# Transposes in place of diagonal products, and GpSimd work in the attention, in a two-layer diffusion backbone

## The chip, the cores and the metric

The kernel runs on one core of a Trainium2 chip. The metric is the device time of one execution in microseconds; smaller is better. Before the change three runs gave a median of 1726.25 us (1725.76 to 1727.16).

## What is computed

Two layers of a diffusion backbone work on 256 latent tokens (one batch) with 256 context tokens as a prefix, 1024 features each, in float32. Each layer is a half-step SwiGLU, a token mixer, and a second half-step SwiGLU. Layer 0 mixes with a bidirectional gated linear recurrence, layer 1 with windowed attention of 16 heads over 4 key heads, with rotary angles and a sink per head.

```python
def rms_norm(x, g):
    return x * rsqrt(mean(x * x, -1) + 1e-6) * g

def modulate(h, g_pre, shift, scale):
    return rms_norm(h, g_pre) * (1 + scale) + shift

def half_ffn_update(h, mod, k, g_pre, g_post, w_in, w_out):
    y = swiglu(modulate(h, g_pre, mod[3*k], mod[3*k+1]), w_in, w_out)
    return h + 0.5 * mod[3*k+2] * rms_norm(y, g_post)

for each layer:
    x, ctx = half_ffn_update(...)            # both streams
    x, ctx = x + gate * rms_norm(mixer(modulate(x, ...), modulate(ctx, ...)), g)
    x, ctx = half_ffn_update(...)            # the last layer: x alone
```

In the attention a softmax over latent keys within a window of 128, all context keys and the sink gives the weights p, and the output is p times the values.

## The kernel before

The 512 tokens lie in four tiles of 128 (0 and 1 context, 2 and 3 latent), always taken in the order 2, 3, 0, 1. The residual `x` lies in SBUF with tokens on the partitions. A matmul wants the features on the partitions, so each tile is normed, turned and modulated before a layer uses it.

**Products in two parts.** A float32 operand is split into a rounded part `hi` (ScalarE, `copy` in L112) and the remainder `lo` (VectorE, subtraction in L113), and each product is the sum of three matmuls (L135 to L137, L150 to L152). Weights arrive by DMA in slots of 128x1024 (`wslot`, L115) and are split the same way; there are 5 slots for raw weights and 8 for split ones.

**Norm and turn.** `mean_sq` (L154) takes the squares' sum on ScalarE and writes the squares into a scratch tile; `rstd` (L159) takes the inverse root in eight tiny VectorE instructions. `diag` (L176) makes a 128x128 diagonal matrix of it, and `turn` (L181) multiplies each 128x128 block of `x` by that diagonal matrix on TensorE, which norms and turns it in one product. The results lie in PSUM, four blocks to a bank. `pre_turn` (L216) applies scale and shift (ScalarE, L225) and splits the result into `hh` and `hl`. `first_turn` (L240) does it for the first layer.

**Boundaries.** After a tile's last output product, `post` (L190) norms the output and adds it to `x`; `pre` (L204) norms the new `x` with high priority and puts off the turning by some matmul units (`DELAY`, `tick`). There are four boundaries with four tiles each, two latent tiles at the end of the attention, and the four tiles of the start: 22 in all.

**The attention** (`attn_mixer`, L718). Eight projection units of 128 query columns, each followed by `rotate` (L757: two products, a permutation matmul and a sum in L768), two of keys, and four tiles of values. Then eight steps: `soft` (L827) computes the scores of four heads, their maximum, exponential and row sums; `mix` (L852) makes four diagonal matrices of the inverse sums (L856), multiplies blocks of the weights by them on TensorE (L861), which scales and turns them, splits the result, and multiplies by the values (L867, L868). The code asks for the scores of step s before the mixing of step s-1. `proj` multiplies by the output weights. GpSimd issues some DMAs and has no arithmetic.

**Order.** The order on each engine is fixed when the program is built, by a scheduler that takes ready instructions by priority. Each engine works through its queue in that order and waits on semaphores.

Of the kernel before, what the change touches and what calls it, by code (L numbers as in the profile page):

```python
# [7 lines left out]
F32 = mybir.dt.float32  # L8
# [3 lines left out]
ALU = mybir.AluOpType  # L12
# [3 lines left out]
P = 128  # L16
# [17 lines left out]
RS = -1.0 / 8192.0  # L34


class Net:
    def __init__(self, ctx, tc):
        self.tc = tc
        self.nc = tc.nc  # L40
        self.ctx = ctx
        self.n = 0
        self.pending = []
        e = ctx.enter_context
        self.const = e(tc.tile_pool(name="const", bufs=1))
        self.big = e(tc.tile_pool(name="big", bufs=1))
        self.rawp = e(tc.tile_pool(name="rawp", bufs=5))
        self.wp = e(tc.tile_pool(name="wp", bufs=8))
        self.sm = e(tc.tile_pool(name="sm", bufs=10))
        self.tp = e(tc.tile_pool(name="tp", bufs=2))  # L50
        self.mmp = e(tc.tile_pool(name="mmp", bufs=4, space=PSUM))
        self.stp = e(tc.tile_pool(name="stp", bufs=4, space=PSUM))
        self.x = self.big.tile([P, 4, D], F32, name="xres")
        self.y = self.big.tile([P, 4, D], F32, name="y")
        self.hh = self.big.tile([P, NK, T], F32R, name="hh")
        self.hl = self.big.tile([P, NK, T], F32R, name="hl")
        self.dh = self.big.tile([P, NK, T], F32R, name="dh")
        self.dl = self.big.tile([P, NK, T], F32R, name="dl")
        self.ph = e(tc.tile_pool(name="ph", bufs=1))
        self.rows = {}  # L60

    def nm(self, s):
        self.n += 1
# [51 lines left out]
    def wslot(self, srcs):  # L115
        nc = self.nc
        raw = self.raw()
        n = 0
        for s in srcs:
            a, b = s.shape[1:]  # L120
            nc.sync.dma_start(raw[:, n : n + a * b].rearrange("p (a b) -> p a b", b=b), s)
            n += a * b
        hi = self.wp.tile([P, D], F32R, tag="whi", name=self.nm("whi"))
        lo = self.wp.tile([P, D], F32R, tag="wlo", name=self.nm("wlo"))
        self.split(hi[:, :n], lo[:, :n], raw[:, :n])
        return hi, lo

    def unit(self, out, w, nk, mh, ml, cols, kb=0, ws=P, wo=0):
# [44 lines left out]
            r = r2  # L173
        return r

    def diag(self, r):  # L176
        dg = self.sm.tile([P, P], F32, tag="diag", name=self.nm("diag"), bufs=2)
        self.nc.vector.tensor_scalar(dg, self.ident, r, RS, op0=ALU.mult, op1=ALU.mult)  # L178
        return dg

    def turn(self, t, b, dg):  # L181
        ps = self.st()
        for q in range(4):
            k = 4 * b + q
            self.nc.tensor.matmul(  # L185
                ps[:, q * P : (q + 1) * P], self.x[:, t, k * P : (k + 1) * P], dg, start=True, stop=True
            )
        return ps

    def post(self, t, ysrc, grow):  # L190
# [10 lines left out]
            nc.vector.scalar_tensor_tensor(tmp, ysrc, r, grow[cond], op0=ALU.mult, op1=ALU.mult)  # L201
        nc.vector.tensor_tensor(self.x[:, t], self.x[:, t], tmp, op=ALU.add)

    def pre(self, t, A, S):  # L204
        with self.tc.high_priority():
            dg = self.diag(self.rstd([self.mean_sq(self.tmp(), self.x[:, t])]))
        self.pending.append([DELAY[t], lambda: self.pre_turn(t, A, S, dg)])

    def tick(self, n):
        for p in list(self.pending):  # L210
# [2 lines left out]
                self.pending.remove(p)  # L213
                p[1]()

    def pre_turn(self, t, A, S, dg):  # L216
        nc = self.nc
        cond = t // 2
        tk = slice(t * P, (t + 1) * P)
        hf = self.tmp()  # L220
        for b in range(2):
            ps = self.turn(t, b, dg)
            for q in range(4):
                k = 4 * b + q
                nc.scalar.activation(  # L225
# [12 lines left out]
        return self.y.rearrange("p a (b t) -> p (a b) t", t=T)  # L238

    def first_turn(self, t):  # L240
        dg = self.diag(self.rstd([self.mean_sq(self.tmp(), self.x[:, t])]))
        for b in range(2):
            ps = self.turn(t, b, dg)
            self.nc.vector.tensor_copy(
                self.turned()[:, 4 * b : 4 * b + 4, t * P : (t + 1) * P], ps.rearrange("p (q c) -> p q c", c=P)
            )
# [183 lines left out]
def net_kernel(  # L430
# [102 lines left out]

        return step

    def boundary(grow, l2, k2, conds=(0, 1)):
        st = {}

        def after(t, ysrc):
            if not st:  # L540
                st["A"] = N.pre_cols(l2, k2, conds)
            with tc.high_priority():
                N.post(t, ysrc, grow)
            N.pre(t, *st["A"])

        return after

# [3 lines left out]
    def ffn(l, k, jobs, l2, k2, mid=None):  # L551
# [19 lines left out]
        1,  # L571
    )
    after_attn = {}
    attn_mixer(
        N,
        attn_w_qkv[0],
# [3 lines left out]
        k_rope,  # L580
        k_mask,
        lambda: after_attn.update(N.load_rows((1, 5), {1: N.x[:, 0]})),
        boundary(after_attn, 1, 2, (1,)),
    )
    last_ffn(N, ffn_w_in[1, 1], ffn_w_out[1, 1], N.load_rows((1, 8), {1: N.x[:, 1]}), out)


# [130 lines left out]
def attn_mixer(N, w_qkv, w_o, sink, k_perm, k_rope, k_mask, rows, after):  # L718
# [38 lines left out]
    def rotate(src):  # L757
# [7 lines left out]
        dst, t = a[:, :HT], a[:, HT:]  # L765
        v.tensor_tensor(dst, src, rope[:, 0], op=ALU.mult)
        v.tensor_tensor(t, pr[:, :HT], rope[:, 1], op=ALU.mult)
        v.tensor_tensor(dst, dst, t, op=ALU.add)  # L768
        return dst

    def qview(i):
# [79 lines left out]

    def mix(u, pts, rs):  # L852
        qt, g = u // NKV, u % NKV
        dg = consts[:, u % 2].rearrange("p (i q) -> p i q", q=P)
        for i in range(4):
            v.tensor_scalar(dg[:, i], N.ident, rs[:, i : i + 1], None, op0=ALU.mult)  # L856
        po = N.st()
        for k in range(4):
            tp = N.st()
            for i in range(4):  # L860
                nc.tensor.matmul(  # L861
                    tp[:, i * P : (i + 1) * P], pts[i][:, k * P : (k + 1) * P], dg[:, i], start=True, stop=True
                )
            ph = N.s2(F32R)
            pl = N.a2(F32R)
            N.split(ph, pl, tp)
# [174 lines left out]
```

## Time and profile before

| what | value |
|---|---|
| median of three runs | 1726.25 us |
| the profiled execution: its time, its span | 1725.57 us, 1723.8 us |
| TensorE busy, weight loads beside it | 1678.0 us (97%), 1425.6 us |
| VectorE busy | 1139.6 us (66%) |
| ScalarE busy | 716.5 us (42%) |
| GpSimd busy | 40.3 us (2%) |
| mean granted TensorE clock | 0.993 |

Busy is the time in which an engine had an instruction under way. Matmuls overlap one another, so the pace of TensorE is read from the distance of their starts. A line of the trace names the code line, the engine and the tiles as out<-in.

### The profile page before, as it was taken

The numbers are of one execution on the slowest core, as the hardware profiler recorded it, in microseconds if no ns is written. First come the engines' busy times: TensorE is split into PE (matmuls) and PEld (weight loads), VectorE is DVE, ScalarE is ACT, GpSimd is POOL, SyncE is SP. The second block draws the span as 40 slices with busy tenths as digits, with TensorE's granted clock in tenths as the row PEclk, the third lists the DMA queues.
The fourth block names the chain that finished last, engine by engine and source line by source line (L and its number), as shares of the span: only waits on it lengthen the run. The fifth ranks groups of instructions, "written<-read, shape, count | busy, mean of one in ns | idle before, by whom it ended". The sixth has DMA issues, their size and how long they took to land.

```text
span 1723.8 us, 23005 instructions
## 1 busy us (share of the span) xinstructions
PE 1678.0 (97%) x8980; PEld 1425.6 (83%) x8980; DVE 1139.6 (66%) x1798; ACT 716.5 (42%) x1148; POOL 40.3 (2%) x82
## 2 busy tenths in 40 slices
PE   5999999999999999999999999999999999999998
PEld 3988888788988798888888898788888887879997
DVE  4947778667878795777833685564433799765554
ACT  3423322225799362333232542322222576564442
POOL 0010000000000001000000001000000000000000
PEclk9999999999999999999999999999999999999999
DMA  9627655453223154666643165765432250047661
GB/s 333 207 92 235 214 171 172 148 170 97 87 86 98 50 192 145 204 190 206 175 119 97 50 190 169 241 220 182 112 106 86 63 181 27 1 141 216 189 188 38
DMA packets 261405, 253.58 MB, mean 147 GB/s; under 512 B 9792, under 2 KB 214040, under 8 KB 261296
## 3 DMA queue, kind: packets, MB, share of 16 engines
q1 hardware_dynamic: 256800, 244.35, 45.6%
q0 software_dynamic: 3456, 6.98, 1.3%
q8 instruction: 70, 1.15, 0.3%
q10 hardware_dynamic: 1040, 0.77, 0.1%
q14 instruction: 39, 0.32, 0.1%
HBM read 250.97 MB, written 1.10 MB: 146 GB/s over the span
## 4 chain that ended last, share of the span: by engine, by line
PE 78%; DVE 9%; ACT 6%; DMA 4%; issue 3%; ACTq 0%; DVEq 0%
PE mm L136 15%; PE mm L135 15%; PE mm L137 15%; PE mm L150 7%; PE mm L152 7%; PE mm L151 7%; DVE m L309 2%; DMA raw<-in_ffn_w_in_dram 2%; DVE wlo L113 2%; PE st L861 2%; PE st L185 1%; ACT tmp L225 1%; ACT whi L112 1%; DMA raw<-in_ffn_w_out_dram 1%; PE st L315 1%
## 5 line engine op out<-in xcount | busy, mean ns | idle before, releaser
L135 PE MATMUL mm<-hh,whi 128*128 128x512 f32 (+1 forms) x1808 | 614.0, 340 | 3.1 <-ACT hh L255 1.6
L136 PE MATMUL mm<-hl,whi 128*128 128x512 f32 (+1 forms) x1808 | 613.4, 340 | 2.0 <-DVE hl L257 1.5
L137 PE MATMUL mm<-hh,wlo 128*128 128x512 f32 (+1 forms) x1808 | 613.5, 340 | 1.0 <-DVE wlo L113 1.0
L112 ACT CAST whi<-raw 128x1024 fp32r<-128x1024 f32 x322 | 331.4, 1038 | 517.5 <-PE mm L136 244.8
L113 DVE TENSOR_TENSOR wlo<-raw,whi 128x1024 fp32r<-128x1024 f32 x322 | 382.6, 1202 | 204.9 <-ACT whi L112 202.2
L135 PEld LDWEIGHTS mm<-hh,whi 128*128 128x128 f32 x1808 | 343.6, 190 | 48.3 <-ACT whi L112 4.2
L136 PEld LDWEIGHTS mm<-hl,whi 128*128 128x128 f32 x1808 | 344.0, 190 | 39.8 <-DVE hl L257 2.1
L137 PEld LDWEIGHTS mm<-hh,wlo 128*128 128x128 f32 x1808 | 344.3, 190 | 38.3 <-DVE wlo L113 1.4
L309 DVE SCALAR_TENSOR_TENSOR m<-raw,cs,m 128x1024 f32<-128x1024 f32 x224 | 278.1, 1279 | 49.1 <-DMA raw<-in_w_mod_dram 37.8
L150 PE MATMUL mm<-whi,dh 128*128 128x512 f32 x592 | 233.3, 394 | 4.7 <-ACT dh L112 2.4
L152 PE MATMUL mm<-whi,dl 128*128 128x512 f32 x592 | 232.1, 392 | 0.4 <-DVE dl L113 0.4
L151 PE MATMUL mm<-wlo,dh 128*128 128x512 f32 x592 | 231.5, 391 | 0.0
L150 PEld LDWEIGHTS mm<-whi,dh 128*128 128x128 f32 x592 | 112.0, 189 | 33.9 <-issue 3.4
L357 DVE TENSOR_TENSOR a<-s,mm 128x512 f32<-128x512 f32 (+1 forms) x96 | 54.4, 567 | 128.2 <-PE mm L137 114.4
L152 PEld LDWEIGHTS mm<-whi,dl 128*128 128x128 f32 x592 | 111.9, 189 | 24.5 <-DVE dl L113 0.8
L151 PEld LDWEIGHTS mm<-wlo,dh 128*128 128x128 f32 x592 | 111.9, 189 | 22.7
L112 ACT CAST dh<-a 128x512 fp32r<-128x512 f32 (+1 forms) x96 | 50.6, 527 | 122.9 <-DVE a L357 122.8
L356 ACT ACTIVATE s<-mm 128x512 f32<-128x512 f32 (+1 forms) x96 | 48.0, 500 | 96.4 <-PE mm L137 96.1
L113 DVE TENSOR_TENSOR dl<-a,dh 128x512 fp32r<-128x512 f32 (+1 forms) x96 | 54.4, 567 | 18.9 <-ACT dh L112 18.6
L225 ACT ACTIVATE tmp<-st,modT,A 128x128 f32<-128x128 f32 x144 | 54.7, 464 | 7.0 <-PE st L185 7.0
L185 PE MATMUL st<-diag,xres 128*128 128x128 f32 x352 | 46.9, 289 | 6.8 <-DVE diag L178 6.2
L185 PEld LDWEIGHTS st<-diag,xres 128*128 128x128 f32 x352 | 44.7, 201 | 10.4 <-issue 6.2
(195 smaller groups left out, 1398.2 us busy)
## 6 DMA issues: line engine op xcount, KB each, us to landing
raw<-in_ffn_w_in_dram SPq DMA_DIRECT2D x176, 512.0 KB, 4.5
raw<-in_w_mod_dram SPq DMA_DIRECT2D x128, 512.0 KB, 4.2
raw<-in_ffn_w_out_dram SPq DMA_DIRECT2D x82, 512.0 KB, 4.5
wm<-in_w_mod_dram SPq DMA_DIRECT2D x16, 512.0 KB, 7.5
raw<-in_rg_w_in_dram SPq DMA_DIRECT2D x16, 512.0 KB, 4.7
raw<-in_attn_w_qkv_dram SPq DMA_DIRECT2D x12, 512.0 KB, 4.1
g<-spill POOLq DMA_DIRECT2D x16, 256.0 KB, 4.1
raw<-in_rg_gate_w_dram SPq DMA_DIRECT2D x16, 256.0 KB, 2.9
```

The costliest lines, as they stand in the source:

```text
L112: self.nc.scalar.copy(hi, src)
L113: self.nc.vector.tensor_tensor(lo, src, hi.bitcast(F32), op=ALU.subtract)
L135: nc.tensor.matmul(out, a, xh, start=(k == 0), stop=False)
L136: nc.tensor.matmul(out, a, xl, start=False, stop=False)
L137: nc.tensor.matmul(out, b, xh, start=False, stop=(k == nk - 1))
L150: nc.tensor.matmul(out, a, wh, start=(k == 0), stop=False)
L151: nc.tensor.matmul(out, a, wl, start=False, stop=False)
L152: nc.tensor.matmul(out, b, wh, start=False, stop=(k == nk - 1))
L185: self.nc.tensor.matmul(ps[:, q * P : (q + 1) * P], self.x[:, t, k * P : (k + 1) * P], dg, start=True, stop=True)
L225: nc.scalar.activation(hf[:, k * P : (k + 1) * P], ps[:, q * P : (q + 1) * P], AF.Identity, bias=S[:, k, cond : cond + 1], scale=A[:, k, c ...
L309: v.scalar_tensor_tensor(acc[c], raw, self.cs[:, k, c : c + 1], acc[c], op0=ALU.mult, op1=ALU.add)
L357: nc.vector.tensor_tensor(b, a, pu, op=ALU.mult)
```

## The change

The tile is scaled by VectorE into a copy and turned by plain transposes, in place of products with a diagonal matrix. At the boundaries the copy goes into `y`, elsewhere into a scratch tile. In the attention, too, transposes take the place of products with diagonal matrices; GpSimd scales the softmax weights in place, subtracts for the remainders `lo` of the weights of that stage, and takes the last sum of the rotation.

```diff
+        self.lo_eng = self.nc.vector
...
-        self.split(hi[:, :n], lo[:, :n], raw[:, :n])
+        nc.scalar.copy(hi[:, :n], raw[:, :n])
+        self.lo_eng.tensor_tensor(lo[:, :n], raw[:, :n], hi[:, :n].bitcast(F32), op=ALU.subtract)
...
-    def diag(self, r):
-        dg = self.sm.tile([P, P], F32, tag="diag", name=self.nm("diag"), bufs=2)
-        self.nc.vector.tensor_scalar(dg, self.ident, r, RS, op0=ALU.mult, op1=ALU.mult)
-        return dg
-
-    def turn(self, t, b, dg):
+    def scaled(self, t, xs):
+        r = self.rstd([self.mean_sq(xs, self.x[:, t])])
+        self.nc.vector.tensor_scalar(xs, self.x[:, t], r, RS, op0=ALU.mult, op1=ALU.mult)
+        return xs
+
+    def turn(self, xs, b):
         ps = self.st()
         for q in range(4):
             k = 4 * b + q
-            self.nc.tensor.matmul(
-                ps[:, q * P : (q + 1) * P], self.x[:, t, k * P : (k + 1) * P], dg, start=True, stop=True
-            )
+            self.nc.tensor.transpose(ps[:, q * P : (q + 1) * P], xs[:, k * P : (k + 1) * P], self.ident)
...
-    def pre(self, t, A, S):
+    def pre(self, t, A, S, buf):
         with self.tc.high_priority():
-            dg = self.diag(self.rstd([self.mean_sq(self.tmp(), self.x[:, t])]))
-        self.pending.append([DELAY[t], lambda: self.pre_turn(t, A, S, dg)])
+            xs = self.scaled(t, buf)
+        self.pending.append([DELAY[t], lambda: self.pre_turn(t, A, S, xs)])
...
     def first_turn(self, t):
-        dg = self.diag(self.rstd([self.mean_sq(self.tmp(), self.x[:, t])]))
+        xs = self.scaled(t, self.tmp())
...
-    def boundary(grow, l2, k2, conds=(0, 1)):
+    def boundary(grow, l2, k2, conds=(0, 1), keep=False):
...
-            N.pre(t, *st["A"])
+            N.pre(t, *st["A"], N.tmp() if keep else N.y[:, t])
...
+    N.lo_eng = nc.gpsimd
     attn_mixer(
...
-        boundary(after_attn, 1, 2, (1,)),
+        boundary(after_attn, 1, 2, (1,), True),
     )
+    N.lo_eng = v
...
-        v.tensor_tensor(dst, dst, t, op=ALU.add)
+        nc.gpsimd.tensor_tensor(dst, dst, t, op=ALU.add)
...
     def mix(u, pts, rs):
         qt, g = u // NKV, u % NKV
-        dg = consts[:, u % 2].rearrange("p (i q) -> p i q", q=P)
         for i in range(4):
-            v.tensor_scalar(dg[:, i], N.ident, rs[:, i : i + 1], None, op0=ALU.mult)
+            nc.gpsimd.tensor_scalar(pts[i], pts[i], rs[:, i : i + 1], None, op0=ALU.mult)
...
-                nc.tensor.matmul(
-                    tp[:, i * P : (i + 1) * P], pts[i][:, k * P : (k + 1) * P], dg[:, i], start=True, stop=True
-                )
+                nc.tensor.transpose(tp[:, i * P : (i + 1) * P], pts[i][:, k * P : (k + 1) * P], N.ident)
```

## Rows read from the trace of the kernel before

**Rows 1.** The page: busy us (share of the span) and instructions, TensorE to GpSimd

```profile
PE 1678.0 (97%) x8980; PEld 1425.6 (83%) x8980; DVE 1139.6 (66%) x1798; ACT 716.5 (42%) x1148; POOL 40.3 (2%) x82
```

**Rows 2.** Windows: us, busy PE, PEld, DVE, ACT, POOL, granted clock, DMA share, GB/s

```profile
0.00:35.00 35.00, 17.31 (x107) 9.72 (x108) 12.88 (x50) 8.00 (x14) 1.33 (x6) 0.94 0.98 338
...
1360.00:1426.00 66.00, 65.33 (x443) 59.20 (x442) 61.13 (x131) 50.70 (x96) 2.17 (x4) 1.00 0.50 160
1426.00:1512.00 86.00, 81.85 (x486) 69.42 (x485) 73.00 (x200) 55.68 (x131) 0.00 (x0) 1.00 0.07 21
```

**Rows 3.** Groups, whole run: line, out<-in, count | busy us, mean ns | idle before

```profile
L185 PE MATMUL st<-diag,xres 128*128 128x128 f32 x352 | 46.9, 289 | 6.8 <-DVE diag L178 6.2 <-issue 0.5
...
L861 PE MATMUL st<-m,y 128*128 128x128 f32 x256 | 35.9, 274 | 0.0
...
L178 DVE TENSOR_SCALAR diag<-ident,small 128x128 f32<-128x128 f32 x22 | 6.3, 286 | 0.5
...
L671 DVE TENSOR_SCALAR g<-g 128x512 f32<-128x512 f32 x16 | 6.1, 423 | 2.2 <-ACT g L669 2.2
...
L686 DVE TENSOR_TENSOR_SCAN g<-m,a 128x512 f32<-128x512 f32 x4 | 4.9, 1218 | 0.0
...
L688 DVE TENSOR_TENSOR_SCAN g<-m,s 128x256 f32<-128x256 f32 x4 | 2.7, 664 | 0.0
...
L795 DVE COPY y<-m 128x256 f32<-128x256 f32 x2 | 0.6, 283 | 0.0
```

**Rows 4.** The chain that ended last: start us, us, what

```profile
13.92 3.67 PE st L185 x16
...
393.18 1.78 PE st L185 x16
...
1439.37 1.11 PE st L861 x10
```

**Rows 5.** Timeline of TensorE at a group of transposes: start us, us

```profile
1207.49 0.60 PE L264 MATMUL st<-ident,s 128*128 128x128 f32 x4
1207.85 0.48 PE L150 MATMUL mm<-whi,dh 128*128 128x512 f32 x1
```

**Rows 6.** Groups of VectorE from 1360 to 1426 us

```profile
L113 DVE TENSOR_TENSOR wlo<-raw,whi 128x1024 fp32r<-128x1024 f32 x18 | 21.7, 1218 | 0.2 <-ACT whi L112 0.2
L786 DVE TENSOR_TENSOR dh<-m,dh 64x256 fp32r<-64x256 f32 x16 | 6.7, 420 | 0.5
L768 DVE TENSOR_TENSOR m<-m 128x256 f32<-128x256 f32 x10 | 4.2, 419 | 0.1
...
L113 DVE TENSOR_TENSOR hl<-tmp,hh 128x512 fp32r<-128x512 f32 x6 | 4.1, 688 | 0.3 <-ACT hh L112 0.2
L805 DVE TENSOR_TENSOR dl<-y,dl 64x512 fp32r<-64x512 f32 x6 | 4.1, 685 | 1.3 <-ACT dl L803 1.3
...
L170 DVE SCALAR_TENSOR_TENSOR small<-small,small 128x1 f32<-128x1 f32 x12 | 2.6, 216 | 0.2
L201 DVE SCALAR_TENSOR_TENSOR tmp<-y,small,g 128x1024 f32<-128x1024 f32 x2 | 2.6, 1286 | 0.1
L202 DVE TENSOR_TENSOR xres<-xres,tmp 128x1024 f32<-128x1024 f32 x2 | 2.4, 1217 | 0.0
...
L172 DVE SCALAR_TENSOR_TENSOR small<-small,small 128x1 f32<-128x1 f32 x12 | 1.9, 158 | 0.3
```

**Rows 7.** Groups of VectorE from 1426 to 1512 us

```profile
L856 DVE TENSOR_SCALAR m<-ident,soft 128x128 f32<-128x128 f32 x32 | 7.7, 279 | 0.1
L113 DVE TENSOR_TENSOR wlo<-raw,whi 128x1024 fp32r<-128x1024 f32 x5 | 6.1, 1217 | 0.0
```

**Rows 8.** Waits from 1426 to 1512 us: us in total, times, longest

```profile
ACT s L112 <- PE st L861: 17.3, 22, 1.7
```

More of the change, by code (lines that the diff above doesn't have):

```diff
@@ L214, in tick, with pre_turn @@
                 p[1]()
-    def pre_turn(self, t, A, S, dg):
+    def pre_turn(self, t, A, S, xs):
         nc = self.nc
@@ L221, in pre_turn @@
         for b in range(2):
-            ps = self.turn(t, b, dg)
+            ps = self.turn(xs, b)
             for q in range(4):
@@ L240, in first_turn @@
     def first_turn(self, t):
-        dg = self.diag(self.rstd([self.mean_sq(self.tmp(), self.x[:, t])]))
+        xs = self.scaled(t, self.tmp())
         for b in range(2):
-            ps = self.turn(t, b, dg)
+            ps = self.turn(xs, b)
             self.nc.vector.tensor_copy(
```

## The prediction

> **What bounds it now.** I read the page's busy shares first: TensorE is busy 1678.0 us of 1723.8, VectorE 1139.6 [rows 1]. In such a kernel a microsecond taken out of TensorE's queue is a microsecond gained, unless TensorE then waits for something else. So I next looked for what TensorE does in the lines the change touches [rows 3], at what pace [rows 4, 5], and then, stage by stage, whether another engine is near its limit [rows 2]. The reader should see there that from 1360 to 1426 us (last tile boundary, projections of the attention) VectorE works 61.1 of 66 us beside TensorE's 65.3, and from 1426 to 1512 us (scores and mixing) 73.0 of 86 beside 81.9. These two stages have two limits at once; elsewhere TensorE has the lead. The profiled execution took 1725.57 us, 0.7 under the median of 1726.25; I make the sum against it and add 0.7.
>
> **Diagonal products become transposes.** Each product has two TensorE instructions in the trace: 22 tiles x 8 products give the 352 of L185, 8 steps x 16 the 256 of L861 [rows 3]. In the chain of waits 16 of L185 take 1.78 us and 10 of L861 1.11 us, 0.111 us each [rows 4]. The transposes that are already there (L264) have one instruction each: four are begun at 1207.49 and the next matmul at 1207.85, 0.09 us each, and I count the 0.111 of the others, the smaller gain [rows 5]. One instruction in two goes.
> - 18 tiles (two context tiles, 16 at boundaries): 18 x 8 x 0.111 = 16.0 us off.
> - The last two tiles, in and behind the attention: 1.8 us off.
> - The mixing: 128 x 0.111 = 14.2 us off. That work is on the path: ScalarE waits 17.3 us for L861 in this stage [rows 8].
> - The first two tiles run at the low level of the clock (3.67 us for 16 instead of 1.78 [rows 4]), so 1.9 us could go in each; but the DMA share is 0.98 in that stretch [rows 2], and what follows waits for loads. Between 0 and 3 us; I take 1.
> Sum: 33.0 us off TensorE's queue.
>
> **Scaling the tile.** The 128x128 diagonal (L178, 286 ns) becomes a 128x1024 tensor_scalar on VectorE. The nearest rows of single-input forms are 283 ns at 256 columns (L795) and 423 at 512 (L671), 0.55 ns a column [rows 3]: 286 + 896 x 0.55 = 0.78 us, 0.49 more per tile. The far bound is a 1024-column instruction with two inputs, 1.29 us (L201 [rows 6]), 1.00 more. Behind it TensorE's first bank of four is ready 0.45 us sooner than with products, so the chain into the next layer keeps its length; and the work lies under the next tile's matmuls except at the last tile. Cover is gone where VectorE is full. I take 1 us for all 22 tiles, bounds 0 and 10. The squares' scratch moving from tmp to y costs nothing: y[t] was read for the last time just before.
>
> **Work moved to GpSimd in the attention.** The trace has no arithmetic on GpSimd, so I bound it. Low end: VectorE's own times, 1.22 us for a weight difference, 0.42 for the rotary sum [rows 6], 0.42 for a 512-column scaling (L671 [rows 3]). High end: the slowest element rate among the elementwise rows, the scan, 1218 ns for 512 columns and 664 for 256 [rows 3], so 2.44, 0.66 and 1.22 us. As the trace shows nothing faster for this engine, I take the high end. The Trainium skill ("GPSIMD Engine Reference", section 3.1) gives 1.96 times VectorE's time for a two-input add; by it a difference would take an estimated 2.4 us, the same sum.
> - 1360 to 1426: 18 differences and 10 sums, 43.9 + 6.6 = 50.5 us of GpSimd in 66. VectorE loses 21.7 + 4.2 us [rows 6] and gains 2 x 0.49: 36 us left. The differences were split far ahead of their use, so 1.2 us more latency is covered; if that lead is used up TensorE waits about a difference, 1.2 us.
> - 1426 to 1512: 32 scalings and the last 2 differences of the output weights (the other 3 of the 5 shown belong to the next layer), 39 + 5 = 44 us in 86. VectorE loses the 32 diagonals, 7.7 us [rows 7], and 2.4: 63 us left. The four scalings stand in series before a step's transposes, 4.9 us instead of 1.1; they lie under the scores of the next head group, as mixing trails the scores by one step. GpSimd's queue also holds the row loads that wait for the residual tiles; those are free sooner now, since the transposes read the copy.
> The relief can remove at most TensorE's idle time in the two stages, 0.7 + 4.1 us. Against that stands a conflict over memory between VectorE and GpSimd, which no row here shows: together bounds of 5 off and 22 on (below). I take 4 on, nearer to the idle time that the rows do show: the order on each engine is planned anew, and the scalings are a new wait.
>
> **Sum:** -33.0 + 1 + 4 = -28; 1725.6 - 28 + 0.7 = **1698 us**.
>
> **Rivals.**
> *VectorE and GpSimd lock each other out for instructions with two inputs in SBUF.* In 1360 to 1426 there are 56 such left on VectorE (L786, hl of L113, L805, L170, L172, L201, L202), 24.4 us in all [rows 6]. If each meets a GpSimd instruction in 50.5/66 of cases and waits half a difference (1.22 us), that is 52 us: 36 + 52 = 88 against 66, so 22 us on, while at half of that nothing is lost. Without the 1.8 us of the stage's own two tiles: 1725.6 - 31 + 1 + 22 - 2 = 1716 us with the rest as in the sum but the small relief. Against it: the 6 output-weight differences in this stage aren't needed until 1460 us and can slip. The Trainium skill ("SBUF — State Buffer", section "Who interferes with whom") states just this exclusion, a whole instruction long; no run here shows it, and by that rule 1716 would come out where I forecast 1698. Chance 0.23.
> *GpSimd costs nothing in the path* and the relief closes the gaps: -33 + 1 - 5: 1689 us. Chance 0.1.
> *Slower: GpSimd and VectorE exclude each other for every instruction.* Place: the two attention stages. Price: 36 + 50.5 = 87 in 66 us and 63 + 44 = 107 in 86, so 42 us on, and the 17.8 us saved in them void: 1726 - 15 + 42 = 1753 us. It decides from the point where both stages together grow by over 15 us. Against it: most of VectorE's time in the second stage goes to instructions that read a matmul result, not SBUF alone. Chance 0.04.
> *The clock falls.* In both stages the granted clock is 1.00, the level of 2.4 GHz [rows 2], with products and a few transposes between full-width matmuls. At 1.2 GHz the remaining 60 us or so of matmul work in the second stage would take 120: 1726 - 17 + 34 = 1743 us. The Trainium skill ("TensorE: Matmul & The Clock Gate", Part 4) says that transposes don't count as TensorE activity for the clock, which speaks against this change; by that rule the mixing would lose what keeps the clock up. The L264 groups here are too short to bear it out, but matmuls stand between all groups. Chance 0.01.
> *A transpose takes two instructions after all*, and nothing changes: 1726 us; against it stands the single instruction of the transposes there now [rows 5]. Chance 0.02.
>
> **How the numbers follow.** A difference under 0.2% (3.5 us) can't be told from none. The forecast has 0.6, over 1690 to 1708 us by its own bounds; the range reaches to 1687 for the free GpSimd and to 1715, most of the way to the lock, leaving out about 0.2. Faster: 0.6 + 0.23 + 0.1 = 0.93; same 0.02, the case without change; slower 0.04 + 0.01 = 0.05.
>
> **What would show it.** Right: 176 instructions of L185's successor and 128 of L861's at 0.11 us; a tile's scaling near 0.78 us; the boundaries nearer together by 3.6 us per layer; the stretch from the first score to the last transpose down from 86 us to 70 to 78; the clock still 1.00. Wrong: VectorE's small instructions (L170, L786) longer or apart while GpSimd works, TensorE waiting for a GpSimd difference or scaling, weight splits late at the boundaries behind the longer scaling. The forecast is wrong above all if the two attention stages don't shrink together by some 12 us.

## The result, and the profile after

The changed kernel takes 1774.6 us (median of 4 runs, 1774.38 to 1778.49) against 1726.0 us for the kernel before on the same chip: a ratio of 1.029, interval 1.0277 to 1.0303. It is 49 us slower where 28 us faster was forecast.

The page's busy shares after, TensorE to GpSimd, beside [rows 1]:

```profile
PE 1672.4 (94%) x8676; PEld 1406.6 (79%) x8676; DVE 1148.0 (65%) x1736; ACT 717.6 (40%) x1148; POOL 146.4 (8%) x144
```

304 matmul instructions have gone (8980 before), as many as counted: 176 of the turns and 128 of the mixing. Yet TensorE is busy only 5.6 us less, in a span that grew by 49 us. Both say that the engine waited, and that part of its work ran at a lower clock. The windows of [rows 2], in the kernel after:

```profile
1360.00:1426.00 66.00, 46.18 (x270) 42.61 (x269) 52.93 (x77) 37.97 (x72) 41.54 (x25) 0.82 0.42 128
1426.00:1512.00 86.00, 67.79 (x339) 52.40 (x338) 53.09 (x121) 43.83 (x99) 46.83 (x30) 0.88 0.13 37
```

TensorE fell from 65.3 to 46.2 us of the 66, and VectorE too is idle more than before. Two engines that both lose busy time are waiting for a third or for each other. The granted clock fell from 1.00 to 0.82 and 0.88.

To find where the 49 us are, I read five marks from the timeline of TensorE in both kernels: the first turn of the first layer boundary, the first turn of the last one, the first score product, the start of the last value product, the end.

| stretch, us | before | after | difference |
|---|---|---|---|
| start to the first boundary | 393.0 | 392.7 | -0.3 |
| layers, up to the last boundary | 953.6 | 957.0 | +3.4 |
| last boundary and projections | 79.9 | 105.9 | +26.0 |
| eight steps of scores and mixing | 87.9 | 109.9 | +22.0 |
| rest | 209.4 | 207.2 | -2.2 |

So there are three things to explain: two losses of over 20 us in the attention, and layers that do not gain though 96 products, two instructions of 0.11 us each, became transposes of one there.

**The new instructions.** Groups of GpSimd, whole run (line, engine, operation, shapes, count | busy us, mean ns | idle before):

```profile
L857 POOL TENSOR_SCALAR y<-y,soft 128x512 f32<-128x512 f32 x32 | 50.2, 1585 | 46.2 <-DVE soft L851 35.2 <-ACT s L113 5.6 <-PE mm L840 5.4
L127 POOL TENSOR_TENSOR wlo<-raw,whi 128x1024 fp32r<-128x1024 f32 x20 | 48.7, 2448 | 120.4 <-ACT whi L126 110.6 <-issue 9.8
...
L770 POOL TENSOR_TENSOR m<-m 128x256 f32<-128x256 f32 x10 | 7.5, 752 | 11.9 <-DVE small L167 5.6 <-DVE m L769 4.1 <-PE mm L139 2.2
```

A difference takes 2.45 us (2.44 counted), a rotary sum 0.75 (0.66 counted), a scaling 1.59 us, above the high end of 1.22.

**The projections.** Groups of VectorE from 1349 to 1456 us:

```profile
L788 DVE TENSOR_TENSOR dh<-m,dh 64x256 fp32r<-64x256 f32 x16 | 17.3, 1082 | 7.0 <-ACT dh L787 6.7
L172 DVE SCALAR_TENSOR_TENSOR small<-small,small 128x1 f32<-128x1 f32 x18 | 13.3, 737 | 0.6
L114 DVE TENSOR_TENSOR hl<-tmp,hh 128x512 fp32r<-128x512 f32 x8 | 8.3, 1038 | 0.7 <-ACT hh L113 0.7
L174 DVE SCALAR_TENSOR_TENSOR small<-small,small 128x1 f32<-128x1 f32 x18 | 8.0, 445 | 0.6
...
L769 DVE TENSOR_TENSOR m<-st,m 128x256 f32<-128x256 f32 x10 | 4.2, 424 | 3.8 <-PE st L766 3.2
L114 DVE TENSOR_TENSOR a<-mm,s 128x256 fp32r<-128x256 f32 x10 | 4.2, 422 | 2.0 <-ACT s L113 1.8
```

Compare the means with [rows 6]: L788 (L786 before) has gone from 420 to 1082 ns, L172 (L170) from 216 to 737, L174 (L172) from 158 to 445, the split into hl from 688 to 1038. These four groups alone grew by 28 us. L769 and the split into `a` have the same operation, but one input is a matmul's result (st, mm); they kept 424 and 422. Of the groups in this stretch only such with both inputs in SBUF got longer, and in them only the instructions that meet one of GpSimd: seven of the 16 of L788 do and take 0.83 to 2.45 us, the other nine 0.42. The timelines of GpSimd and of VectorE show why (start us, us, instruction):

```profile
1378.28 7.05 POOL L127 TENSOR_TENSOR wlo<-raw,whi 128x1024 fp32r<-128x1024 f32 x3
```

```profile
1379.39 0.15 DVE L169 TENSOR_SCALAR small<-small 128x1 int32<-128x1 int32 x1
1379.58 5.77 DVE L172 SCALAR_TENSOR_TENSOR small<-small,small 128x1 f32<-128x1 f32 x1
1385.39 0.16 DVE L174 SCALAR_TENSOR_TENSOR small<-small,small 128x1 f32<-128x1 f32 x1
1385.58 0.22 DVE L172 SCALAR_TENSOR_TENSOR small<-small,small 128x1 f32<-128x1 f32 x1
```

An instruction on 128 numbers, 0.22 us long elsewhere, lasts 5.77 us. It begins 1.3 us into a row of three GpSimd differences and ends when the third does; GpSimd is not slowed. The one-input instruction ahead of it (L169) passed in 0.15 us in the midst of the first difference.

What TensorE waits for from 1349 to 1456 us (us in total, times, longest) is VectorE above all; it has no wait for a GpSimd difference there:

```profile
PE st L766 <- DVE a L114: 11.1, 4, 5.4
PE st L187 <- DVE y L180: 7.4, 2, 4.2
```

ScalarE waits 10.0 us for GpSimd's rotary sums, where it waited 4.2 for VectorE's. The rotary sum was not moved by itself in any run; with the differences alone on GpSimd (below) ScalarE waits 10.2 us for VectorE's sums, so the longer wait needs no sum on GpSimd.

**The steps.** Waits from 1456 to 1566 us (us in total, times, longest), beside [rows 8]:

```profile
ACT s L113 <- PE st L862: 31.2, 17, 6.7
PEld st L862 <- POOL y L857: 26.5, 21, 3.1
PE st L862 <- POOL y L857: 19.0, 20, 2.7
```

TensorE waits 19 us for GpSimd's scalings, and ScalarE, which needs the transposes next, waits 31.2 us where it waited 17.3. Four scalings of 1.59 us in series are 6.3 us ahead of a step's transposes.

**The layers.** TensorE at the end of a boundary (timeline):

```profile
630.04 0.28 PE L139 MATMUL mm<-hh,wlo 128*128 128x256 f32 x1
631.99 1.09 PE L187 MATMUL st<-ident,y 128*128 128x128 f32 x8 [1.67 <-DVE y L180]
635.10 1.22 PE L137 MATMUL mm<-hh,whi 128*128 128x256 f32 x4 [2.01 <-ACT hh L113]
...
637.66 0.41 PE L138 MATMUL mm<-hl,whi 128*128 128x256 f32 x1
637.87 0.41 PE L139 MATMUL mm<-hh,wlo 128*128 128x256 f32 x1
...
641.84 0.28 PE L137 MATMUL mm<-hh,whi 128*128 128x256 f32 x1
641.96 0.28 PE L138 MATMUL mm<-hl,whi 128*128 128x256 f32 x1
```

It waits 1.67 us for the scaled tile and 2.01 us for what follows the turn. Behind these waits the products come 0.21 us apart, and from 641.71 us 0.12 us. The windows of these stretches give a granted clock of 0.53 and then 1.00:

```profile
637.00:642.00 5.00, 5.00 (x25) 5.00 (x26) 2.87 (x3) 0.08 (x1) 0.00 (x0) 0.53 0.51 152
642.00:650.00 8.00, 8.00 (x70) 8.00 (x68) 4.35 (x5) 3.65 (x5) 0.00 (x0) 1.00 0.54 167
```

So these waits cost more again behind them, in work at the lower level of the clock (1.2 in place of 2.4 GHz).

### The profile page after: what moved, and what is told of

Its sections match the earlier page's. It is cut to its first block, busy times and chain, and to the rows that moved or that the text cites. A ratio compares the mean times of both kernels' runs of the same rounds, so it can differ in the third digit from the quotient of the medians.

```text
span 1772.7 us, 22478 instructions
## 1 busy us (share of the span) xinstructions
PE 1672.4 (94%) x8676; PEld 1406.6 (79%) x8676; DVE 1148.0 (65%) x1736; ACT 717.6 (40%) x1148; POOL 146.4 (8%) x144
## 5 line engine op out<-in xcount | busy, mean ns | idle before, releaser
L127 DVE TENSOR_TENSOR wlo<-raw,whi 128x1024 fp32r<-128x1024 f32 (+1 forms) x302 | 358.5, 1200 | 207.5 <-ACT whi L126 205.1
L137 PEld LDWEIGHTS mm<-hh,whi 128*128 128x128 f32 x1808 | 348.9, 194 | 52.7 <-ACT hh L113 4.5
L138 PEld LDWEIGHTS mm<-hl,whi 128*128 128x128 f32 x1808 | 348.7, 193 | 39.3 <-DVE hl L114 1.3
L139 PEld LDWEIGHTS mm<-hh,wlo 128*128 128x128 f32 x1808 | 348.6, 193 | 38.0 <-DVE wlo L127 0.9
L127 POOL TENSOR_TENSOR wlo<-raw,whi 128x1024 fp32r<-128x1024 f32 x20 | 48.7, 2448 | 120.4 <-ACT whi L126 110.6
L857 POOL TENSOR_SCALAR y<-y,soft 128x512 f32<-128x512 f32 x32 | 50.2, 1585 | 46.2 <-DVE soft L851 35.2
```

Of the source, the lines that this page charges most:

```text
L127: self.lo_eng.tensor_tensor(lo[:, :n], raw[:, :n], hi[:, :n].bitcast(F32), op=ALU.subtract)
L137: nc.tensor.matmul(out, a, xh, start=(k == 0), stop=False)
L138: nc.tensor.matmul(out, a, xl, start=False, stop=False)
L139: nc.tensor.matmul(out, b, xh, start=False, stop=(k == nk - 1))
L857: nc.gpsimd.tensor_scalar(pts[i], pts[i], rs[:, i : i + 1], None, op0=ALU.mult)
```

## The experiments

Four kernels split the change; only the rotary sum is in none of them alone. The theory going in: GpSimd's differences lock VectorE; its scalings are late; the turns' gain is lost in waits for VectorE.

**The turns alone.**

```
 after.py, with the attention of before:
-    N.lo_eng = nc.gpsimd
-        nc.gpsimd.tensor_tensor(dst, dst, t, op=ALU.add)
+        v.tensor_tensor(dst, dst, t, op=ALU.add)
 and mix() as before (diagonal products)
```

> The tile turns alone: scaled copy and transposes at the 22 tiles; the attention as before, nothing on GpSimd. Theory (the boundary's chain through VectorE sets when the last tile can be turned, so TensorE waits for what it saves): no gain, 1722 to 1732 us, with TensorE waiting over 1 us before the turn of the last context tile at three or more boundaries. Rival (TensorE's queue sets the time at the boundaries, and the loss in the changed kernel comes back from elsewhere): 1726 - 18 = 1708 us.

1737.6 us against 1726.6, ratio 1.0065 (1.0046 to 1.0083): slower than even the theory had it (1722 to 1732). The layers took 959.1 us in place of 953.6.

**The weight differences alone.**

```
 before.py, wslot():
-        self.split(hi[:, :n], lo[:, :n], raw[:, :n])
+        nc.scalar.copy(hi[:, :n], raw[:, :n])
+        self.lo_eng.tensor_tensor(lo[:, :n], raw[:, :n], hi[:, :n].bitcast(F32), op=ALU.subtract)
 and N.lo_eng = nc.gpsimd in the attention
```

> The kernel before with the weight differences of the attention on GpSimd, and nothing else of the change. Lock theory (a VectorE instruction with two inputs in SBUF stands still while GpSimd reads SBUF, through a whole run of its instructions): slower by 12 to 28 us, with L170, L172 and L786 of 2 us and more among those that meet a difference, and the projections stage longer by most of that. Rival (GpSimd is merely slow, and what waits for a difference is late): slower by 0 to 4 us, VectorE's small instructions at their old times, TensorE waiting for wlo.

1756.2 us, 1.0175 (1.0157 to 1.0192): 29.5 us, a little over the theory's range. The steps kept their length, and the last boundary and projections grew from 79.9 to 108.4 us. No engine waits for a GpSimd difference in that stretch; TensorE's longest wait, 9.8 us, is for VectorE. The lock is longer still than in the changed kernel:

```profile
1381.46 12.52 DVE L172 SCALAR_TENSOR_TENSOR small<-small,small 128x1 f32<-128x1 f32 x1
...
1384.65 9.31 POOL L127 TENSOR_TENSOR wlo<-raw,whi 128x1024 fp32r<-128x1024 f32 x4
```

The instruction on 128 numbers ends with the fourth of these differences, 0.02 us apart; a fifth ran ahead of them. The rival, lateness, is ruled out here.

**The mixing alone.**

```
 before.py, mix():
-            v.tensor_scalar(dg[:, i], N.ident, rs[:, i : i + 1], None, op0=ALU.mult)
+            nc.gpsimd.tensor_scalar(pts[i], pts[i], rs[:, i : i + 1], None, op0=ALU.mult)
 and transposes of pts[i] in place of the products with dg
```

> The kernel before with the mixing's products replaced by transposes and the weights scaled by GpSimd; tile turns, weight differences and rotary sums as before. Theory (four scalings of 1.57 us in series stand before each step's transposes and are not covered): slower by 5 to 22 us in the steps, with TensorE waiting for the scalings over 25 us in all. Rival (the steps grow in the changed kernel by what came over from the projections stage): faster by 5 to 14 us, since TensorE has 14.2 us less to do.

1746.9 us, 1.0117 (1.0097 to 1.0137). The steps took 110.5 us in place of 87.9, so the whole loss of 20 us lies in them, as the theory had it. TensorE waited 21.1 us for the scalings, somewhat less than the 25 expected. The three parts alone (11, 29.5 and 20 us) add up to more than the 49 of the change.

**All transposes, no arithmetic on GpSimd.**

```
 after.py, with N.lo_eng and the rotary sum on VectorE, and in mix():
-            nc.gpsimd.tensor_scalar(pts[i], pts[i], rs[:, i : i + 1], None, op0=ALU.mult)
+            v.tensor_scalar(pts[i], pts[i], rs[:, i : i + 1], None, op0=ALU.mult)
```

> All transposes of the change, at the tiles and in the mixing, but no arithmetic on GpSimd: VectorE scales the weights (about 0.48 us each in place of a 0.28 us diagonal), and takes differences and rotary sums as before. Theory (GpSimd alone makes the change slow; at the boundaries nothing is gained): 1712 to 1722 us, the steps shorter by 6 to 14 us and the rest as with the turns alone. Rival (VectorE sets the steps, and its 6 us more of scaling eat the gain): 1726 to 1734 us.

1733.5 us, 1.0045 (1.0027 to 1.0062); the theory's 1712 to 1722 was missed and the rival's 1726 to 1734 met. So GpSimd's share of the change is 1774.6 - 1733.5 = 41 us. The steps took 89.5 us though 14 us of TensorE work had gone. The window of 1435 to 1525 us holds them, to be read beside the last line of [rows 2]:

```profile
1435.00:1525.00 90.00, 77.96 (x377) 57.33 (x375) 81.02 (x203) 58.54 (x133) 0.00 (x0) 0.98 0.13 37
```

VectorE is now busy longer than TensorE, 81.0 us of 90: a scaling of 512 columns takes it 480 ns where a diagonal took 279.

### What locks VectorE

Four kernels leave the arithmetic of before as it is, and let GpSimd do work behind each of the 20 weight splits of the attention that nothing reads. So no one waits for its result; what can still be late is the release of the weights that it reads. `h` is the rounded half of the weights.

```
 before.py, wslot(), behind the split:
+            for q in range(3):
+                nc.gpsimd.tensor_tensor(dup, h[:, q * 256 : q * 256 + 256], h[:, q * 256 : q * 256 + 256], op=ALU.subtract)
```

> The kernel before, with work added that nobody waits for: in the attention GpSimd takes, behind each of the 20 weight splits (which stay on VectorE), three differences of 256 columns of the rounded weights with themselves into a tile that nothing reads. So GpSimd is busy with reads of SBUF as in the changed kernel (some 40 to 50 us), but nothing is late because of its result. Theory (a lock: VectorE's instructions with two SBUF inputs stand still while GpSimd reads): between 1347 and 1426 us the small instructions with two SBUF inputs (0.216 us before), the table products (0.420) and the splits (0.688, 1.218) take longer, the evictions from PSUM (0.42) do not; 1734 to 1752 us. Rival (only the lateness of GpSimd's differences cost the 26 us in the changed kernel): every VectorE mean as before, 1724 to 1730 us.

1743.9 us, 1.0091 (1.0076 to 1.0106). Groups of VectorE and GpSimd, 1347 to 1440 us:

```profile
L114 DVE TENSOR_TENSOR wlo<-raw,whi 128x1024 fp32r<-128x1024 f32 x18 | 25.0, 1395 | 0.0
L793 DVE TENSOR_TENSOR dh<-m,dh 64x256 fp32r<-64x256 f32 x16 | 8.7, 542 | 0.5
L114 DVE TENSOR_TENSOR hl<-tmp,hh 128x512 fp32r<-128x512 f32 x8 | 7.1, 892 | 0.9 <-ACT hh L113 0.9
L175 DVE SCALAR_TENSOR_TENSOR small<-small,small 128x1 f32<-128x1 f32 x21 | 6.7, 320 | 0.5
...
L774 DVE TENSOR_TENSOR m<-st,m 128x256 f32<-128x256 f32 x10 | 4.1, 417 | 1.2 <-PE st L771 1.1
...
L130 POOL TENSOR_TENSOR dup<-whi 128x256 f32<-128x256 f32 x54 | 52.7, 976 | 115.4 <-ACT whi L113 111.6
```

Every group with two inputs in SBUF is longer than in [rows 6], those with one from a matmul are not. The waits of this stretch name GpSimd for no engine. So the lock is shown without any wait for GpSimd, but weaker than in the change: 542 ns against 1082 for the table products, and 16 us against 29.5, with GpSimd busy about as long (53 us). Why it is weaker was not tried; the instructions are shorter here, and take both inputs from one tile.

```
-                nc.gpsimd.tensor_tensor(dup, h[...], h[...], op=ALU.subtract)
+                nc.gpsimd.memset(dup, 0.0)
```

> As the run before it, but GpSimd only fills the same unread tile with zeros, three times 256 columns behind each weight split: it writes SBUF and reads nothing. If the lock comes with GpSimd's reads (or with its two reads at once), VectorE's durations stay as in the kernel before and the time is 1724 to 1731 us; if any GpSimd work in SBUF holds VectorE up, the small instructions take longer than 0.216 us here too, and the time is 1731 to 1745 us.

1727.1 us, 1.000 (0.999 to 1.0009), but it tells nothing: the fills depended on nothing and ran at the program's start. So they were tied to their place by a scaling of one column ahead of them:

```
+            nc.gpsimd.tensor_scalar(dup[:, 0:1], h[:, 0:1], 2.0, None, op0=ALU.mult)
+            for q in range(8):
+                nc.gpsimd.memset(dup, 0.0)
```

> The fill of e6m_memset tied to its place: behind each weight split GpSimd scales one column of the rounded weights (so that it can't begin earlier) and then fills the unread tile eight times with zeros, 8 x 0.312 us by the fills of e6m_memset, about 2.7 us a split as in the changed kernel. If reads make the lock, VectorE's means stay within 10% of before and the time is 1723 to 1732 us. If writes do too, the small instructions lengthen to over 0.25 us and the time is 1735 to 1752 us.

1728.0 us, 1.0004 (0.9995 to 1.0013). GpSimd filled for 50 us here, and VectorE's instructions with two inputs did not notice:

```profile
L794 DVE TENSOR_TENSOR dh<-m,dh 64x256 fp32r<-64x256 f32 x16 | 6.7, 420 | 0.5
...
L176 DVE SCALAR_TENSOR_TENSOR small<-small,small 128x1 f32<-128x1 f32 x19 | 4.1, 218 | 0.4
...
L131 POOL MEMSET dup<- 128x256 f32 x160 | 50.1, 313 | 9.0
```

```
-                nc.gpsimd.tensor_tensor(dup, h[...], h[...], op=ALU.subtract)
+                nc.gpsimd.tensor_scalar(dup, h[...], 2.0, None, op0=ALU.mult)
```

> As e6_dup, but each unread GpSimd instruction has one input in place of two: 256 columns of the rounded weights times two. If the lock comes with two inputs on GpSimd, VectorE's small instructions keep their 0.216 and 0.158 us, the table products 0.420, and the time is 1723 to 1730 us. If any read of SBUF by GpSimd locks VectorE's two-input instructions, these lengthen as in e6_dup (0.320, 0.248, 0.542) or more, since a scaling took 1.59 us for 512 columns, and the time is 1736 to 1752 us.

1732.9 us, 1.0037 (1.0023 to 1.0051), between the two cases: the table products took 474 ns, the splits into hl 786, the small instructions 247 and 168. One input locks too, but less than two, though GpSimd was busy for longer (59 instructions of 1109 ns). ScalarE waited 3.9 us here for a tile that GpSimd still read, so not all of the 5.5 us need be the lock; with the fills it waited 5.8 us in all, and that cost nothing.

Two inputs on VectorE are not the whole condition. Some with one input in SBUF were held up as well where they met GpSimd. In the kernel with the weight differences alone, a diagonal that takes 0.29 us elsewhere stood still beside a GpSimd difference that ran from 1376.24 us for 2.35 us:

```profile
1376.25 2.42 DVE L180 TENSOR_SCALAR diag<-ident,small 128x128 f32<-128x128 f32 x1
```

A copy of 128x256 took 0.70 us beside the unread differences and 0.32 and 0.43 beside the fills, in place of 0.28. One-input instructions on one column kept their 0.15 us.

### Why the turns gain nothing

**Turned by a product with the identity**, the tile scaled as in the change:

```
 e1_turns, turn():
-            self.nc.tensor.transpose(ps[...], xs[:, k * P : (k + 1) * P], self.ident)
+            self.nc.tensor.matmul(ps[...], xs[:, k * P : (k + 1) * P], self.ident, start=True, stop=True)
```

> The turns with the tile scaled beforehand on VectorE as in the changed kernel, attention as before, but turned by a product with the identity (0.222 us a block) in place of a transpose (0.109): 176 blocks, 19.9 us more TensorE time than with the turns alone (1737.6 us). If the transposes' saving was worth its TensorE time and the scaling is what cost, this is 1750 to 1758 us. Theory (TensorE only waits for VectorE's chain, the saving is wait at most boundaries): about half of it or less shows, 1736 to 1748 us.

1732.9 us, 1.0037 (1.0023 to 1.0051), below the theory's range of 1736 to 1748: 20 us more of TensorE work cost nothing at all. TensorE doesn't set the time of these stages.

VectorE's timeline in the boundary shows what does. In the kernel with the turns alone, between the steps of one root:

```profile
414.85 0.14 DVE L167 TENSOR_SCALAR small<-small 128x1 f32<-128x1 f32 x1
...
416.70 0.21 DVE L172 SCALAR_TENSOR_TENSOR small<-small,small 128x1 f32<-128x1 f32 x1
416.83 1.22 DVE L127 TENSOR_TENSOR wlo<-raw,whi 128x1024 fp32r<-128x1024 f32 x1
417.97 0.15 DVE L174 SCALAR_TENSOR_TENSOR small<-small,small 128x1 f32<-128x1 f32 x1
418.04 1.22 DVE L127 TENSOR_TENSOR wlo<-raw,whi 128x1024 fp32r<-128x1024 f32 x1
...
422.44 1.22 DVE L127 TENSOR_TENSOR wlo<-raw,whi 128x1024 fp32r<-128x1024 f32 x1
423.58 0.74 DVE L180 TENSOR_SCALAR y<-xres,small 128x1024 f32<-128x1024 f32 x1
```

The eight tiny steps need 1.7 us where nothing comes between (the root ahead of this one); they are spread from 414.85 to 423.58, since six weight differences of 1.22 us stand between them in the engine's order. In the kernel before the same root ran from 414.73 to 418.11, with one weight difference and one other split in between. The tile is turned at 424.4 us there and at 418.5 before.

**The last turn later.**

```
-DELAY = {2: 5, 3: 5, 0: 5, 1: 5}
+DELAY = {2: 5, 3: 5, 0: 5, 1: 7}
```

> The turns of the tiles as in the changed kernel, everything else as before (1737.6 us in its run), with the turn of the last tile of a stage (tile 1) placed 7 units later in TensorE's order in place of 5. Theory (VectorE's chain sets when the tile can be turned, TensorE comes too early and waits 2 to 3.5 us at each boundary, and runs at the lower clock behind the wait): other products fill the wait, the waits in front of the transposes of tile 1 fall under 1 us, 1724 to 1734 us. Rival (what follows needs the turned tile at once, so that the wait only moves behind it): 1735 to 1744 us.

1732.6 us, 1.0037 (1.0023 to 1.0051). This kernel takes two groups of products of tile 1 ahead of its turn, on what the buffer held before, so its time has less waiting in it than the computation allows, and it still is not faster than before. TensorE's waits for turned tiles in the layers did not shrink either (9.8 us, 8.9 in the turns alone), where the theory had them under 1 us for tile 1.

**The root kept together by a rule of order**, in the turns alone and, as a control, in the kernel before:

```
 wslot():
+        with self.order(self.last):
             self.lo_eng.tensor_tensor(lo[:, :n], ...)
 with self.last set to the scaling (the diagonal) of the tile turned last
```

> The turns of the changed kernel with attention as before (1737.6 us in its run), and one rule of order more: a weight difference written behind a tile's scaling in the program is queued behind that scaling on VectorE, so that it can't stand between the eight steps of the root. Theory (the loss of the turns is made by the order on VectorE: in the boundary at 405 to 440 us six weight differences of 1.22 us stand between the steps of one root): the steps of the root stand together, tile 0 is scaled by about 418 us and not at 424, and the time falls by 6 to 16 us, to 1722 to 1731 us. Rival (the differences only get in where nothing else is ready, and their delay makes the products wait for weights): 1735 to 1745 us.

> The kernel before with the same rule of order (a weight difference behind the diagonal tile of the last tile's root). Control for the run before it: theory, the roots of the kernel before stand nearly together already (two weight differences between the steps of the third at 414 to 418 us), so the rule changes little, 1723 to 1730 us. Rival (the rule is worth as much to any kernel): 1712 to 1721 us.

1760.5 us, 1.0196 (1.0179 to 1.0214), and 1767.1 us, 1.0229 (1.0203 to 1.0256): both worse, and outside all four ranges. The control is not quite the same edit: there the rule holds back the whole split, ScalarE's rounding too. In the first the tile was scaled at 416.4 and turned at 418.3 us, as expected. But the differences that products in hand needed were now behind the next tile's root too, and TensorE waited 8.8 us for the next turn:

```profile
PE st L189 <- DVE y L182: 8.8, 1, 8.8
```

TensorE's waits for turned tiles in the layers were 23.2 us in the first and 19.2 in the second. VectorE's order has to serve both; moving the wait is no cure.

**A shorter root**, two Newton iterations in place of three, in the turns alone and in the kernel before (the root is less exact then):

```
-RS = -1.0 / 8192.0
+RS = 1.0 / 16.0
...
-        for c in (-3.0, -12.0, -768.0):
+        for c in (-3.0, -12.0):
```

> The turns of the changed kernel with attention as before, with two Newton iterations of the root in place of three (six steps on VectorE in place of eight, 0.38 us of work fewer at each root; the scale constant goes with it). Theory (each link of the chain lets a weight difference of 1.22 us in): the boundaries come up to 2 us earlier, 1726 to 1734 us. Rival (it is not the length of the chain): 1735 to 1740 us.

> The kernel before with two Newton iterations of the root in place of three. Control for the run before it: theory, the turns of the kernel before wait less for VectorE, so this gives 0 to 4 us, 1722 to 1727 us. Rival (as much as with the transposes): 1716 to 1721 us.

1707.0 us, 0.9891 (0.9868 to 0.9914), with the turns: 30 us less than with three iterations. 1716.8 us, 0.9939 (0.9918 to 0.996), in the kernel before: 10 us less. Both gained more than the theory gave them (1726 to 1734, 1722 to 1727). With the turns, 18.7 us came in the layers, 4.7 ahead of them and 5.5 behind the steps. TensorE's waits for the tile to be turned from 380 to 1350 us, with three iterations, then with two:

```profile
PE st L187 <- DVE y L180: 6.9, 3, 3.4
...
PE st L187 <- DVE small L169: 2.0, 1, 2.0
```

```profile
PE st L187 <- DVE y L180: 1.4, 2, 1.1
```

The clock shows it as well: the boundary around 580 to 650 us in the kernel before, in the turns alone with three iterations, and, from 571 to 641 us, with two:

```profile
580.00:650.00 70.00, 69.70 (x482) 64.86 (x481) 58.38 (x115) 40.52 (x84) 0.00 (x0) 1.00 0.42 133
```

```profile
580.00:650.00 70.00, 63.60 (x402) 58.01 (x401) 56.15 (x111) 38.12 (x80) 0.00 (x0) 0.95 0.40 122
```

```profile
571.00:641.00 70.00, 69.76 (x485) 64.97 (x484) 58.60 (x103) 40.80 (x85) 0.00 (x0) 1.00 0.47 144
```

TensorE has 69.8 of 70 us again, at the full clock. The waits for turns fell by 7.5 us only; over the whole run the mean granted clock rose from 0.985 to 0.996, which is worth 19 us at most (an estimate: 1735.0 x 0.015 less 1706.9 x 0.004).

**Product in place of transpose, with the shorter root.**

```
 e10_scaled_product, with the two lines of e14_turns_two
```

> The tile scaled beforehand, but turned by a product with the identity, with two Newton iterations. With three iterations this was 1732.9 us, no slower than with transposes (1737.6). Theory (there the saving of the transposes went into waits for the root; with the shorter root TensorE sets the time and the saving shows): 1712 to 1727 us, over 5 us more than the 1707.0 with transposes. Rival (the scaling and its order, not the transposes, made the gain of 20 us over the kernel before): 1704 to 1710 us.

1731.3 us, 1.0022 (1.0008 to 1.0036): 24 us more than with transposes, above the range given. With three iterations the same exchange gave nothing. So the transposes gain their TensorE time (19.5 us counted) once VectorE is not late; the other 4 us are not accounted for. The medians, from four chips on which the kernel before took 1726.6 to 1727.5:

| turn | three iterations | two |
|---|---|---|
| product with the diagonal | 1726.6 | 1716.8 |
| scaled tile, product with the identity | 1732.9 | 1731.3 |
| scaled tile, transpose | 1737.6 | 1707.0 |

### The parts together

> All transposes of the change, the softmax weights scaled on VectorE, no arithmetic on GpSimd (1733.5 us in its run), with two Newton iterations of the root. Theory (the shorter root takes the waits off the boundaries as with the turns alone, which fell by 30 us; the mixing's transposes bring 2 to 6 us more, since its steps are not bound by TensorE): 1698 to 1707 us. Rival (the transposes of the mixing add VectorE work that costs as much as it brings): 1707 to 1712 us.

```
 e4_no_pool, with the two lines of e14_turns_two
```

1708.5 us, 0.9896 (0.9881 to 0.9911): the same as the turns alone with the shorter root (1707.0), so the mixing's transposes bring nothing here, as the rival had it (1707 to 1712). These two are the fastest kernels of this case; the kernel before with the shorter root (1716.8) comes next.

> The changed kernel (1774.6 us) with two Newton iterations. Theory (the boundaries in front of the attention lose their waits as with the turns alone, some 15 to 20 us, and the lock and the scalings in series on GpSimd stay, some 22 us each in the attention): 1748 to 1760 us. Rival (the shorter root takes the waits off the attention too): 1715 to 1740 us.

```
 after.py, with the two lines of e14_turns_two
```

1751.6 us, 1.0143 (1.0126 to 1.016), as the theory had it. The layers took 941.4 us (957.0 in the changed kernel), the projections 105.1 and the steps 110.5. GpSimd's work costs 1751.6 - 1708.5 = 43 us here, and 41 with the longer root: its price doesn't hang on the boundaries.

## Why the prediction was wrong

**What bounds it: the step that failed first.** "A microsecond taken out of TensorE's queue is a microsecond gained, unless TensorE then waits for something else" was right, and the clause was the case. "Elsewhere TensorE has the lead" was the step that failed. I took the busy share of 97% as a proof of it for all layers and looked for a second limit only in the attention. The lead was there before the change (69.7 of 70 us in the boundary above), but it was small: VectorE's root must be done before the turn, and with less work on TensorE and a longer scaling the root came too late, with 8.9 us of waits in the layers and a lower clock behind them. Of the 17.8 us counted for the turns (less scaling) nothing was left, and 11 us were lost on top. The shorter root brought them out: the exchange of product and transpose then gave 24 us, where 176 x 0.111 = 19.5 were counted.

**Scaling the tile: mis-sized.** 0.78 us for one was right (0.75 measured). "The work lies under the next tile's matmuls" was not: with the same products the scaling beforehand cost 5.4 us (1732.9 against 1727.5), and with the shorter root 14.5 (1731.3 against 1716.8), for 1 us taken and a bound of 10. What hides 0.5 us of duration does not hide a new order on the engine. Which part of the 14.5 is the order and which the length was not tried.

**The mixing: the term of 14.2 us was wrong.** The wait of ScalarE for L861 was read as proof that these products are on the path. They were, but VectorE was not far from its own limit, 73.0 of 86 us [rows 2]: with VectorE scaling, the steps kept their length (87.9 us before, 89.5 and, with the shorter root, 86.6 after). That VectorE alone holds them there was not tried.

**GpSimd: the bounds were too narrow.** +4 was taken, -5 to 22 given, and it was 41 to 43, about half from the lock in the projections and half from the scalings in the steps. The difference was priced right, the scaling too low: the slowest elementwise row of VectorE was no high end for another engine, which needs 3.1 ns a column with one input and 2.4 with two. That the differences' own latency is covered was right: TensorE never waited for one in the projections. I put the scalings "under the scores of the next head group"; TensorE waited 19 us for them.

**The rival that came true, in its mechanism and not in its time.** VectorE and GpSimd locking each other out got a chance of 0.23 and a price of 22 us; the projections grew by 26.0 us, the differences alone cost 29.5, and the unread differences 16. Its 1716 us was far off all the same, as it kept the transposes' gain and left out the scalings. Half a difference was taken for a wait; the longest were 5.77 and 12.52 us. It was rated low for want of a row, with a written rule at hand: the Trainium skill ("SBUF — State Buffer", "Who interferes with whom") states that a VectorE instruction with two SBUF inputs contends with GpSimd's reads and not with its writes. These runs agree in each part: 542 ns for 420 with reads, 420 with fills, 417 with one input from a matmul. My objection, that the output-weight differences can slip, was beside the point, as the lock asks for overlap and not for need.

**The other rivals.** The clock did fall, to 0.82 and 0.88, but behind waits and not for want of products: with all transposes and no GpSimd work it was 0.98 in the steps, and 1.00 with the shorter root. Exclusion for every instruction did not come: VectorE instructions that read a matmul's result kept their times, and so did those with one input of one column; but scalings and copies with one input were held up too (2.42 us for a diagonal). That rival's 1753 us lay nearest to the result, for another reason.

**What would show it.** Of the signs of being right, the instruction counts and the scaling of a tile held. Those of being wrong came: the lengthened L170 and L786, TensorE's waits for the scalings, and two attention stages that grew by 48 us where they had to shrink by 12.

## What to carry to other kernels

Before work is moved to GpSimd beside a busy VectorE, count VectorE's instructions with two inputs in SBUF, and its scalings and copies there: each may stand still through a row of GpSimd's reads, however small it is. A busy share of 97% is no proof that each microsecond of an engine counts: at every place where the engine's order meets another engine's chain, look when that chain ends, for in these runs a wait there cost clock behind it too. When a saving doesn't show, shorten the chain it runs into: the same transposes were worth nothing with eight steps in the root and 24 us with six.

## What the runs showed that was not expected

- The lock reaches over several GpSimd instructions: 5.77 us for a VectorE instruction on 128x1, through the rest of three differences, and 12.52 us with the differences alone.
- GpSimd's one-input scaling is slower per column than its two-input difference: 1585 ns for 512 columns against 2448 for 1024. Its fill of 256 columns took 313 ns.
- Two steps fewer in each root, 0.45 us by the starts of the steps, brought 30 us in one kernel and 10 in the other, where all 42 roots together got 19 us shorter. The order on VectorE is planned anew with every edit; a part of such gains and losses belongs to that order and not to the instruction edited.
